# Fused transformer layer on one core: weight sums in place, side work spread over the attention stage, loads and stores begun a turn later

## The chip, the cores and the metric

The kernel is one launch on one core of a Trainium2 chip, written with a library that places tiles in pools, adds the semaphores and sets the order of instructions on each engine. Engines are named as in the profile: PE (matrix unit) and its weight loads (PEld), DVE (vector), ACT (scalar, activations), POOL (general purpose) and SP, whose queue issues nearly all DMAs. Each engine, and SP's queue, takes its instructions strictly in order: one that waits holds those behind it. The metric is the device time in microseconds (us), compared by the median of several runs.

## What is computed

One encoder layer over a sequence of 1024 positions of width 1024, in float32, with a conditioning vector c:

```python
mod = silu(c) @ w_ada + b_ada                    # six rows: sh1, sc1, g1, sh2, sc2, g2
h = layer_norm(x) * (1 + sc1) + sh1
q_a, k_a, v_a, f_a, q_c, k_c, v_c, gate_a, gate_c = split(h @ w_in)
o_a = forgetting_attention(q_a, k_a, v_a, f_a + b_f)      # 8 heads, causal
o_c = chunk_band_attention(q_c, k_c, v_c, rel_bias)       # 8 heads, a band of 9 chunks
mix = (sigmoid(gate_a) * (o_a @ w_br_fox) + sigmoid(gate_c) * (o_c @ w_br_chunk)) @ w_out
x = layer_norm(alpha * x + (1 + g1) * mix, ln1_g, ln1_b)
h = layer_norm(x) * (1 + sc2) + sh2
a, val = split(causal_depthwise_conv(h @ w_up, conv_w, conv_b))
x = layer_norm(alpha * x + (1 + g2) * ((silu(a) * val) @ w_down), ln2_g, ln2_b)
```

## The kernel before

Products in float32 are made of three matmuls: each operand is split into a rounded part and a remainder (`wh` and `wl` for weights; ACT makes `wh`, POOL makes `wl`, lines 103 and 104, from a loaded `ws`, line 96). The products with w_up and w_down are made with seven products of blocks instead of eight (Strassen's scheme), which needs sums and differences of weight blocks.

**The stage that the change touches** is attention, from about 114 us, when its first side loads are issued, to about 775 us. Eight pairs of heads are gone through in the order of a table `plan`: first the chunk branch (pairs 4 to 7), then the forgetting branch (2, 3, 0, 1). Per pair there are eight steps (two heads, four groups of queries): `scores` (PE `pss`, then DVE adds a bias and takes the minimum, line 477, then ACT's exponential, line 483), `probs` (PE transposes into `pst`, line 517; ACT and DVE split the result into two parts `pt`, lines 520 and 521), `weighted` (PE `pso`). `prep` readies the next head: it loads swapped key halves (`m2`, lines 420 and 421) and a bias tile. For the chunk branch this is `cb` (line 427), which DVE scales at once (line 428), and in which POOL then sets two corners; for the forgetting branch it is `fb` (line 424), from which POOL makes masked diagonal blocks `fm` (line 443).

Between these steps PE works on units of a `Stream`: projections of later heads (`psq`, `psv`) and the gates (`psg`, stored as `gd`). `step` advances the stream by about 2.6 us of PE work; one call is one turn.

Beside that run two generators, advanced a piece at a time:
- `beside`: the late modulation rows (`ada_late`, eight half rows). Each has eight pieces: load `wa` (256 KB, line 179), ACT multiplies by one value of the condition (183), POOL adds to `acc` (185), and at the end PE sums over partitions (`psada`).
- `aside`: `up_sums` for 8 pairs of blocks of w_up and `down_sums` for 11 pairs of rows of w_down, 19 units. Each loads two tiles `dr` of 512 KB (lines 567 and 550), POOL makes four sums or differences of 128x512 (573 and 555), and four stores of 256 KB go to scratch in HBM (`wd`, lines 576 to 578; `td`, lines 558 and 560). The later stages load them.

What sets the order: the library runs through the written order and places each instruction as early as its engine, its operands and its buffers let it by its own estimates, so that side work is often far ahead of where it is written. On the chip that order is fixed.

After the stage, `load_o` reads the attention outputs (`ost`), multiplies by inverted softmax sums (`ort`) and splits them (`oh`, ACT, line 758; `ol`, DVE, 759) for the merge with the gates (`psb`).

Of the kernel before, what the change touches and what calls it, by code (L numbers as in the profile page):

```python
# [42 lines left out]
def body(ctx, tc, a, out):  # L43
# [128 lines left out]
    def ada_late(v, half, pieces, accs, psum):  # L172

        acc = None
        ws = []
        for k in range(KD + 1):
            if k < KD:
                ws.append(pieces())
                sy.dma_start(out=ws[k], in_=ada_src(v, half * H, H)[:, k : k + 1, :])
            if k > 0:  # L180
                acc = acc or accs()
                w = ws[k - 1][:, 0, :]
                se.mul(out=acc if k == 1 else w, in_=w, mul=cond[:, k - 1 : k])
                if k > 1:
                    po.tensor_tensor(out=acc, in0=acc, in1=w, op=ALU.add)
            yield
        ps = psum()
        ada_sums(ps, acc, H)
        yield
        ada_bias(ps, v, half * H, H, v != 3)  # L190

# [57 lines left out]
    class Stream:  # L249
# [32 lines left out]
        def step(self):  # L282
            unit = self.units[self.cur]
            if self.gen is None:
                self.prime(self.cur)
                self.gen = unit.run(self.ready.pop(self.cur, []))
            cost = next(self.gen, None)
            if cost is None:
                self.live -= len(unit.parts)
                self.gen = None  # L290
                self.cur += 1
                cost = 0.0
            else:
                self.split()
            self.load()
            return cost
# [11 lines left out]
    qk = {}  # L308

# [85 lines left out]
    def unit_g():  # L395
        gi = next(gates)

        def run(ws):
            wh, wl = ws[0]
            for half in range(2):  # L400
# [8 lines left out]
                sy.dma_start(out=gd[half, gi], in_=sg)  # L409
# [128 lines left out]
    def mod(v, half):  # L538
        return ada_late(
            v, half, lambda: ap.tile([P, 1, H], F32, name=nm("wa"), tag="wa", bufs=2),  # L540
            lambda: ap.tile([P, H], F32, name=nm("acc"), tag="acc", bufs=1),
            lambda: pmm.tile([P, H], F32, name=nm("psada"), tag="mm"),
        )

    def down_sums():

        for i in range(NPAIR):
            rows = [ap.tile([P, D], F32, name=nm("dr"), tag=f"dr{r}", bufs=1) for r in range(2)]
            for r in range(2):
                sy.dma_start(out=rows[r], in_=a["w_down"][order[2 * i + r]])  # L550
            yield
            (b11, b12), (b21, b22) = [[w[:, halves(n)] for n in range(2)] for w in rows]
            t1, t3 = [ap.tile([P, H], F32, name=nm("dt"), tag=f"dt{r}", bufs=1) for r in range(2)]
            for j, (dst, x, y) in enumerate(((t1, b12, b11), (t3, b22, b12), (b22, b22, t1), (b21, b21, b22))):
                po.tensor_sub(out=dst, in0=x, in1=y)
                yield
                if j != 2:
                    sy.dma_start(out=td[i, (0, 2, 1, 3)[j]], in_=dst)
                    if j == 3:
                        sy.dma_start(out=td[i, 1], in_=b22)  # L560

    def up_sums():

        for c in range(HEAD):
            cols = [ap.tile([P, D], F32, name=nm("dr"), tag=f"dr{b}", bufs=1) for b in range(2)]
            for b in range(2):
                sy.dma_start(out=cols[b].rearrange("p (k n) -> p k n", k=KD), in_=a["w_up"][2 * c + b])
            yield
            (w11, w12), (w21, w22) = [[w[:, halves(n)] for n in range(2)] for w in cols]
            s1, s2 = [ap.tile([P, H], F32, name=nm("dt"), tag=f"dt{r}", bufs=1) for r in range(2)]  # L570
            for j, (dst, x, y, op) in enumerate(((s1, w21, w22, ALU.add), (s2, s1, w11, ALU.subtract),
                                                 (w11, w11, w21, ALU.subtract), (w12, w12, s2, ALU.subtract))):
                po.tensor_tensor(out=dst, in0=x, in1=y, op=op)
                yield
                if j in (0, 3):
                    sy.dma_start(out=wd[c, j], in_=dst)
            sy.dma_start(out=wd[c, 1], in_=s2)
            sy.dma_start(out=wd[c, 2], in_=w11)
# [111 lines left out]
    beside = chain(*(mod(v, half) for v in (2, 4, 3, 5) for half in range(2)))  # L690
    aside = chain(up_sums(), down_sums())
    ticks = 0
    for u, (ip, _) in enumerate(plan):
# [5 lines left out]
        for n in range(8 * u, 8 * u + 8):  # L699
# [3 lines left out]
            for qt in range(2):  # L703
# [17 lines left out]
            if i == 1 and g % 2 == 1:  # L721
                sy.dma_start(out=od[g // 2, ip], in_=o_now.pop((ip, g // 2)))
# [12 lines left out]
        if u % 2:  # L735
            inverted(ip - 1)
    for _ in chain(beside, aside):
        pass
# [7 lines left out]
    def load_o(half, pool, tag, bufs, rpool, rtag):  # L746
        os_ = {}
        for i in (4, 6, 2, 0):
# [13 lines left out]
        return os_  # L762

    o0 = load_o(0, ap0, "qs", 4, ap0, "m1")
    stream.finish(len(stream.units))
    es.close()
# [23 lines left out]
    def summed(c, j, pool, tag):  # L790
# [596 lines left out]
```

## Time and profile before

| | us |
|---|---|
| median of 3 runs | 1668.33 (1667.33 to 1672.18) |
| the profiled execution | 1665.98 |
| its span, first to last instruction | 1663.8 |
| PE busy | 1540.7 (93%) |
| DVE / ACT / POOL busy | 1041.0 / 790.8 / 593.4 |
| mean granted PE clock | 0.965 of full speed |
| DMA queue of SP | 264.42 MB, 47.3% of 16 engines' span |

Busy times of engines overlap, so they don't add up to the span. An engine's idle time counts only where the engine that sets the pace waits for it. In a row on a wait the engine named behind the arrow is the one whose event came last by the profile. The granted clock is what PE was given: at half clock a matmul takes almost twice as long. A DMA's time to landing runs from its issue to the arrival of all its data.

### The profile page before, as it was taken

The numbers are of one execution on the slowest core, as the hardware profiler recorded it, in microseconds if no ns is written. First come the engines' busy times: TensorE is split into PE (matmuls) and PEld (weight loads), VectorE is DVE, ScalarE is ACT, GpSimd is POOL, SyncE is SP. The second block draws the span as 40 slices with busy tenths as digits, with TensorE's granted clock in tenths as the row PEclk, the third lists the DMA queues.
The fourth block names the chain that finished last, engine by engine and source line by source line (L and its number), as shares of the span: only waits on it lengthen the run. The fifth ranks groups of instructions, "written<-read, shape, count | busy, mean of one in ns | idle before, by whom it ended". The sixth has DMA issues, their size and how long they took to land. (4 is left out here: it accounts for less than half of the span.)

```text
span 1663.8 us, 22257 instructions
## 1 busy us (share of the span) xinstructions
PE 1540.7 (93%) x7693; PEld 1290.5 (78%) x7693; DVE 1041.0 (63%) x2053; ACT 790.8 (48%) x1420; POOL 593.4 (36%) x455
## 2 busy tenths in 40 slices
PE   6899888887999999998889897899999999999996
PEld 3788777777988988887777675788888888888885
DVE  6746444434544545453758978577777877855688
ACT  3446544534555555553223535454544455456451
POOL 1126545645243242422204364545445445100000
PEclk9999989998999999999989898899999999999998
DMA  9037766676243244523763625443344232597552
GB/s 360 26 98 237 241 226 215 207 233 204 65 140 102 83 129 125 152 89 123 237 214 139 246 93 185 171 145 134 114 171 152 90 108 83 188 383 239 184 198 79
DMA packets 120449, 274.83 MB, mean 165 GB/s; under 512 B 12689, under 2 KB 21585, under 8 KB 120337
## 3 DMA queue, kind: packets, MB, share of 16 engines
q1 hardware_dynamic: 115056, 264.42, 47.3%
q10 hardware_dynamic: 4752, 7.17, 1.2%
q0 software_dynamic: 528, 1.84, 0.3%
q8 instruction: 60, 0.98, 0.2%
q14 instruction: 53, 0.43, 0.1%
HBM read 197.51 MB, written 67.47 MB: 159 GB/s over the span
## 5 line engine op out<-in xcount | busy, mean ns | idle before, releaser
L104 POOL TENSOR_TENSOR wl<-ws,wh 128x1024 fp32r<-128x1024 f32 x54 | 131.5, 2439 | 250.5 <-ACT wh L103 247.7
L816 PE MATMUL psu<-hc,wx 128*128 128x512 f32 x720 | 168.4, 389 | 0.0
L816 PEld LDWEIGHTS psu<-hc,wx 128*128 128x128 f32 x720 | 135.1, 188 | 28.1
L1052 DVE SCALAR_TENSOR_TENSOR pcv<-u,convp,pcv 128x1024 f32<-128x1024 f32 x88 | 113.2, 1286 | 45.4 <-ACT pcv L1050 44.4
L1193 DVE TENSOR_TENSOR op<-rw,op 128x512 fp32r<-128x512 f32 x146 | 93.5, 688 | 52.8 <-ACT op L1192 52.5
L1192 ACT CAST op<-rw 128x512 fp32r<-128x512 f32 x146 | 85.3, 622 | 83.1 <-PE psd L1205 39.5
L520 ACT CAST pt<-pst 128x512 fp32r<-128x512 f32 (+1 forms) x192 | 82.1, 451 | 74.1 <-PE pst L517 72.5
L521 DVE TENSOR_TENSOR pt<-pst,pt 128x512 fp32r<-128x512 f32 (+1 forms) x192 | 96.9, 520 | 30.0 <-ACT pt L520 28.4
L1204 PE MATMUL psd<-op,op 128*128 128x512 f32 x292 | 113.7, 389 | 0.9 <-DVE op L1193 0.9
L1203 PE MATMUL psd<-op,op 128*128 128x512 f32 x292 | 113.6, 389 | 0.0
L1205 PE MATMUL psd<-op,op 128*128 128x512 f32 x292 | 113.6, 389 | 0.0
L517 PE MATMUL pst<-ident,s 128*128 128x128 f32 x528 | 84.8, 280 | 28.5 <-DVE pt L521 28.5
L483 ACT ACTIVATE s<-s,mx 128x640 f32<-128x640 f32 (+7 forms) x128 | 94.4, 737 | 33.3 <-DVE mx L477 31.7
L228 PE MATMUL psq<-h1h,wl 128*128 128x512 f32 x256 | 103.9, 406 | 5.6 <-POOL wl L104 5.6
L226 PE MATMUL psq<-h1h,wh 128*128 128x512 f32 x256 | 107.6, 421 | 0.4 <-DVE h1h L222 0.4
L227 PE MATMUL psq<-h1l,wh 128*128 128x512 f32 x256 | 104.2, 407 | 1.8 <-DVE h1l L223 1.8
L226 PE MATMUL psg<-h1h,wh 128*128 128x512 f32 x256 | 105.3, 411 | 0.0
L228 PE MATMUL psg<-h1h,wl 128*128 128x512 f32 x256 | 101.0, 395 | 0.0
L227 PE MATMUL psg<-h1l,wh 128*128 128x512 f32 x256 | 100.9, 394 | 0.0
L531 PE MATMUL pso<-pt,vs 128*128 128x256 f32 x608 | 91.2, 288 | 4.2 <-DVE pt L521 3.1
L103 ACT CAST wh<-ws 128x1024 fp32r<-128x1024 f32 x54 | 56.3, 1046 | 76.7 <-PE psq L227 16.5
L517 PEld LDWEIGHTS pst<-ident,s 128*128 128x128 f32 x528 | 64.7, 144 | 35.3 <-DVE pt L521 28.5
(268 smaller groups left out, 4007.0 us busy)
## 6 DMA issues: line engine op xcount, KB each, us to landing
ws<-in_w_up SPq DMA_DIRECT2D x36, 512.0 KB, 3.7
wa<-in_w_ada SPq DMA_DIRECT2D x64, 256.0 KB, 3.3
dr<-in_w_down SPq DMA_DIRECT2D x22, 512.0 KB, 4.6
rw<-td SPq DMA_DIRECT2D x44, 256.0 KB, 4.6
yd<-y SPq DMA_DIRECT2D x20, 512.0 KB, 2.8
rw<-yd SPq DMA_DIRECT2D x40, 256.0 KB, 4.0
rw<-sd SPq DMA_DIRECT2D x33, 256.0 KB, 4.6
wa<-in_w_ada SPq DMA_DIRECT2D x8, 1024.0 KB, 10.8
```

Source lines behind the costliest of these rows:

```text
L104: po.tensor_sub(out=lo, in0=st, in1=hi)
L226: pe.matmul(ps, wh, xh, start=start, stop=False)
L227: pe.matmul(ps, wh, xl, start=False, stop=False)
L228: pe.matmul(ps, wl, xh, start=False, stop=stop)
L483: se.activation(out=st[:, 0:nk], in_=st[:, 0:nk], func=AF.Exp, scale=-1.0, bias=prev, accum_out=sums[:, col : col + 1])
L517: pe.transpose(ps[:, b * P : (b + 1) * P], st[:, c0 : c0 + P], ident)
L521: ve.tensor_sub(out=dl, in0=src, in1=dh)
L816: pe.matmul(ps, w[:, a_, k, :], h[k][b_], start=first, stop=k == 3 and a_ == 1, skip_group_check=on)
L1052: ve.scalar_tensor_tensor(out=ps, in0=u[b][:, 2 - d : S + 2 - d], scalar=cp[:, 2 - d : 3 - d], in1=ps, op0=ALU.mult, op1=ALU.add)
L1203: pe.matmul(ps[t], g[:, 0, ts], d[:, 0], start=start, stop=False, skip_group_check=on)
L1204: pe.matmul(ps[t], g[:, 0, ts], d[:, 1], start=False, stop=False, skip_group_check=on)
L1205: pe.matmul(ps[t], g[:, 1, ts], d[:, 0], start=False, stop=stop, skip_group_check=on)
```

## The change

- The sums of one unit are made in place in one tile `dr` of 128x4x512, by a common generator `four`; after the four sums one store of 1 MB takes all of it. The sums stand in another order in `wd` and `td`, and the readers' indices follow.
- `late_modulation` replaces `ada_late`: one generator over all 64 pieces, with loads issued two pieces ahead.
- Each turn advances both side generators (before, one of them), and both have turns in which nothing is issued, between a load and its first use and behind a store.
- Stores of gates (`gd`) and of attention outputs (`od`) are put on a list and issued at the next turn. In `step` the next weight's load comes ahead of the split of the one before, and both come a turn apart.
- Five mask buffers `fm` instead of three.
- `load_o` takes a list of pairs of heads; the last pair is read after the last gate unit.

```diff
             if cost is None:
...
                 cost = 0.0
+                self.load()
             else:
+                self.load()
                 self.split()
-            self.load()
             return cost
...
+    stores = []
+
+    def begun():
+        while stores:
+            stores.pop(0)()
...
-                sy.dma_start(out=gd[half, gi], in_=sg)
+                stores.append(partial(sy.dma_start, out=gd[half, gi], in_=sg))
...
-            fm = ap.tile([P, P], F32, name=nm("fm"), tag="fm", bufs=3)
+            fm = ap.tile([P, P], F32, name=nm("fm"), tag="fm", bufs=5)
...
+    def late_modulation():
+
+
+        pieces = [(v, half, k) for v in (2, 4, 3, 5) for half in range(2) for k in range(KD)]
+        ws = {}
+
+        def load(n):
+            if n < len(pieces):
+                v, half, k = pieces[n]
+                ws[n] = ap.tile([P, 1, H], F32, name=nm("wa"), tag="wa", bufs=2)
+                sy.dma_start(out=ws[n], in_=ada_src(v, half * H, H)[:, k : k + 1, :])
+
+        load(0)
+        yield
+        load(1)
+        yield
+        yield
+        for n, (v, half, k) in enumerate(pieces):
+            w = ws.pop(n)[:, 0, :]
+            if k == 0:
+                acc = ap.tile([P, H], F32, name=nm("acc"), tag="acc", bufs=1)
+                se.mul(out=acc, in_=w, mul=cond[:, 0:1])
+            else:
+                se.mul(out=w, in_=w, mul=cond[:, k : k + 1])
+                po.tensor_tensor(out=acc, in0=acc, in1=w, op=ALU.add)
+            yield
+            load(n + 2)
...
+            yield
+
+    def four(steps, srcs, dst):
+
+        x = ap.tile([P, 4, H], F32, name=nm("dr"), tag="dr", bufs=1)
+        for r in range(2):
+            sy.dma_start(out=x[:, 2 * r : 2 * r + 2, :], in_=srcs[r])
+        yield
+        yield
+        yield
+        for n, (o, p, q, op) in enumerate(steps):
+            po.tensor_tensor(out=x[:, o, :], in0=x[:, p, :], in1=x[:, q, :], op=op)
+            if n:
+                yield
+        sy.dma_start(out=dst.rearrange("j p n -> p j n"), in_=x)
+        yield
+        yield
...
-            t1, t3 = [ap.tile([P, H], F32, name=nm("dt"), tag=f"dt{r}", bufs=1) for r in range(2)]
-            for j, (dst, x, y) in enumerate(((t1, b12, b11), (t3, b22, b12), (b22, b22, t1), (b21, b21, b22))):
-                po.tensor_sub(out=dst, in0=x, in1=y)
-                yield
-                if j != 2:
-                    sy.dma_start(out=td[i, (0, 2, 1, 3)[j]], in_=dst)
-                    if j == 3:
-                        sy.dma_start(out=td[i, 1], in_=b22)
...
+            yield from four(((0, 1, 0, sub), (1, 3, 1, sub), (3, 3, 0, sub), (2, 2, 3, sub)), srcs, td[i])
...
                     spent += stream.step()
-                    ticks += 1
-                    if ticks % 2 or next(beside, aside) is aside:
-                        next(aside, None)
+                    begun()
+                    next(beside, None)
+                    next(aside, None)
...
-    o0 = load_o(0, ap0, "qs", 4, ap0, "m1")
+
+    o0, o1 = {}, {}
+    load_o(0, o0, (4, 6, 2), ap0, "qs", 4, ap0, "m1")
     stream.finish(len(stream.units))
+    begun()
+    load_o(0, o0, (0,), ap0, "qs", 4, ap0, "m1")
```

How the instructions stand on the engines at three places. First, SP around the load of the last chunk bias tile (`cb`), before and then after; a number at a name's end tells one buffer's use from another.

```order
L558 DMA td<-dr_6598 128x512
L550 DMA dr_6979<-in_w_down 128x1024
L722 DMA od<-o_521_2709 128x512
L550 DMA dr_6980<-in_w_down 128x1024
L558 DMA td<-dt_7020 128x512
L420 DMA m_709_3555<-qm_2891 64x1024
L409 DMA gd<-sg_3230 128x512
L96 DMA ws_3285<-in_w_v 128x1024
L421 DMA m_709_3555<-qm_2891 64x1024
L427 DMA cb_3558<-in_rel_t 128x640
L409 DMA gd<-sg_3302 128x512
L558 DMA td<-dt_7021 128x512
```

```order
L563 DMA dr_4862<-in_w_down 128x1024 x2
L295 DMA od<-o_514_2708 128x512
L571 DMA td<-dr_4862 128x4x512
L295 DMA gd<-sg_3225 128x512
L97 DMA ws_3298<-in_w_v 128x1024
L535 DMA wa_3390<-in_w_ada 128x512
L535 DMA wa_3505<-in_w_ada 128x512
L407 DMA m_699_3553<-qm_2886 64x1024
L295 DMA gd<-sg_3296 128x512
L408 DMA m_699_3553<-qm_2886 64x1024
L414 DMA cb_3556<-in_rel_t 128x640
L535 DMA wa_3603<-in_w_ada 128x512
```

Two modulation loads moved ahead of the bias load, and of the side work around it one store of 1 MB is left. On DVE the scaling of that tile stands here, before and after:

```order
L536 TENSOR_TENSOR o_573_2934<-pso_3309,ot_3322 64x256
L428 TENSOR_SCALAR cb_3558<-cb_3558 128x640
L521 TENSOR_TENSOR pt_3325<-pst_3335,pt_3325 128x4x128
L521 TENSOR_TENSOR pt_3326<-pst_3342,pt_3326 128x128
L477 ISA s_3361,mx_3365<-pss_3362,cb_3187 128x256
L477 ISA mx_3365 128x1
L521 TENSOR_TENSOR pt_3325<-pst_3369,pt_3325 128x3x128
```

```order
L523 TENSOR_TENSOR o_562_2928<-pso_3303,ot_3316 64x256
L508 TENSOR_TENSOR pt_3319<-pst_3329,pt_3319 128x4x128
L508 TENSOR_TENSOR pt_3320<-pst_3336,pt_3320 128x128
L464 ISA s_3356,mx_3360<-pss_3357,cb_3182 128x256
L464 ISA mx_3360 128x1
L508 TENSOR_TENSOR pt_3319<-pst_3364,pt_3319 128x3x128
L415 TENSOR_SCALAR cb_3556<-cb_3556 128x640
```

The scaling moved behind three evacuations of transposed scores (`pt`) and the score pass between them.

Second, SP at the last unit of the weight sums, before and after (`ws<-in_w_g` are gate weights, `fb<-fd` the bias tiles of the forgetting branch; the `fb` in the first piece is the second of eight, that in the second piece the third).

```order
L179 DMA wa_4683<-in_w_ada 128x512
L558 DMA td<-dr_7903 128x512
L560 DMA td<-dr_7903 128x512
L722 DMA od<-o_690_3463 128x512
L420 DMA m_893_4454<-qm_3642 64x1024
L421 DMA m_893_4454<-qm_3642 64x1024
L424 DMA fb_4457<-fd 128x1024
```

```order
L563 DMA dr_6788<-in_w_down 128x1024
L571 DMA td<-dr_6788 128x4x512
L563 DMA dr_7051<-in_w_down 128x1024 x2
L97 DMA ws_4566<-in_w_g 128x1024
L571 DMA td<-dr_7051 128x4x512
L411 DMA fb_4903<-fd 128x1024
L408 DMA m_980_4900<-qm_4503 64x1024
```

The last store of the sums moved from ahead of the second `fb` to ahead of the third, and the load of a unit's tile follows the store of the unit before.

Third, ACT at the end of the stage, before and after (`sg` the last two gates, `oh` the split of the last pair of attention outputs, `wh` weights of the merge).

```order
L408 ACTIVATE sg_7991<-psg_7966 128x512
L103 CAST wh_8104<-ws_8102 128x1024
L758 CAST oh_7962<-ost_7956 128x1024
L408 ACTIVATE sg_8019<-psg_7994 128x512
L103 CAST wh_8145<-ws_8143 128x1024
```

```order
L395 ACTIVATE sg_7867<-psg_7842 128x512
L104 CAST wh_7990<-ws_7988 128x1024
L395 ACTIVATE sg_7894<-psg_7869 128x512
L766 CAST oh_7904<-ost_7898 128x1024
L104 CAST wh_8031<-ws_8029 128x1024
```

The last gate moved ahead of the cast of the attention output.

More of the change, by code (lines that the diff above doesn't have):

```diff
@@ L1 @@
 import math
+from functools import partial
 from itertools import chain, count, cycle
@@ L536, in weighted @@
         ve.tensor_tensor(out=o32[own, g % 2 * 256 : (g % 2 + 1) * 256], in0=ps[own, 0:256], in1=tmp[own, :], op=ALU.add)
[L538 to L543, printed above, removed]
+    def late_modulation():
[21 more added lines that the diff above has]
+            load(n + 2)
+            if k == KD - 1:
+                ps = pmm.tile([P, H], F32, name=nm("psada"), tag="mm")
+                ada_sums(ps, acc, H)
+                yield
+                ada_bias(ps, v, half * H, H, v != 3)
+            yield
@@ L545, in down_sums @@
     def down_sums():
+        sub = ALU.subtract
         for i in range(NPAIR):
[L548 to L552, printed above, removed]
-            t1, t3 = [ap.tile([P, H], F32, name=nm("dt"), tag=f"dt{r}", bufs=1) for r in range(2)]
-            for j, (dst, x, y) in enumerate(((t1, b12, b11), (t3, b22, b12), (b22, b22, t1), (b21, b21, b22))):
-                po.tensor_sub(out=dst, in0=x, in1=y)
-                yield
-                if j != 2:
-                    sy.dma_start(out=td[i, (0, 2, 1, 3)[j]], in_=dst)
-                    if j == 3:
-                        sy.dma_start(out=td[i, 1], in_=b22)
+            srcs = [a["w_down"][order[2 * i + r]].rearrange("p (j n) -> p j n", j=2) for r in range(2)]
+            yield from four(((0, 1, 0, sub), (1, 3, 1, sub), (3, 3, 0, sub), (2, 2, 3, sub)), srcs, td[i])
@@ L562, in up_sums @@
     def up_sums():
+        sub = ALU.subtract
         for c in range(HEAD):
[L565 to L578, printed above, removed]
+            srcs = [a["w_up"][2 * c + b].rearrange("p (j k) n -> p j (k n)", j=2) for b in range(2)]
@@ L581, in body @@
+            yield from four(((3, 2, 3, ALU.add), (2, 0, 2, sub), (0, 3, 0, sub), (1, 1, 0, sub)), srcs, wd[c])
     plan = [
@@ L689, in body @@
     done = len(first_units)
-    beside = chain(*(mod(v, half) for v in (2, 4, 3, 5) for half in range(2)))
+    beside = late_modulation()
     aside = chain(up_sums(), down_sums())
-    ticks = 0
     for u, (ip, _) in enumerate(plan):
@@ L744, in body, with load_o @@
     o_cm, op_ = opened(name="o", bufs=1, side="right")
-    def load_o(half, pool, tag, bufs, rpool, rtag):
-        os_ = {}
-        for i in (4, 6, 2, 0):
+    def load_o(half, os_, pairs, pool, tag, bufs, rpool, rtag):
+        for i in pairs:
             st = pool.tile([P, 2, H], F32, name=nm("ost"), tag=tag, bufs=bufs)
@@ L788, in raw, with summed @@
         return raws[c, b]
-    def summed(c, j, pool, tag):
-        if (c, j) not in raws:
+    def summed(c, sl, pool, tag):
+        if (c, sl.start) not in raws:
             st = pool.tile([P, 2, H], F32, name=nm("ws"), tag=tag, bufs=2)
-            sy.dma_start(out=st, in_=wd[c, j : j + 2].rearrange("j p n -> p j n"))
-            raws[c, j] = [st[:, i, :].rearrange("p (k n) -> p k n", k=4) for i in range(2)]
-        return raws[c, j]
+            sy.dma_start(out=st, in_=wd[c, sl].rearrange("j p n -> p j n"))
+            raws[c, sl.start] = [st[:, i, :].rearrange("p (k n) -> p k n", k=4) for i in range(2)]
+        return raws[c, sl.start]
     def operand(slot, tmp, x, y=None, op=None, eng=ve, lo=po):
@@ L1013, in body @@
     turned_1(x1)
-    start = summed(order[0], 0, hbp, "fs"), raw(order[1], 1, hbp, "fs")
+    start = summed(order[0], slice(0, 4, 3), hbp, "fs"), raw(order[1], 1, hbp, "fs")
     g2row = g1p.tile([P, D], F32, name="g2row", tag="g1row")
```

30 lines of the change are left out of this document (7 added, 23 removed).

## Prediction

> **What bounds the kernel now.** I read the page first, then the busy time by stage, then PE's waits in the one stage where side work runs, then two of its stalls in order of time.
>
> ```profile
> span 1663.8 us, 22257 instructions
> PE 1540.7 (93%) x7693; PEld 1290.5 (78%) x7693; DVE 1041.0 (63%) x2053; ACT 790.8 (48%) x1420; POOL 593.4 (36%) x455
> PEclk9999989998999999999989898899999999999998
> ```
>
> PE is the bound, 1540.7 of 1663.8 us. What a rearrangement can win is PE's idle time, and the slow clock that shows up beside it. By stage (columns: length, then busy us of PE, PEld, DVE, ACT, POOL, then granted clock, DMA share, GB/s):
>
> ```profile
> 114.00:459.00 345.00, 304.31 (x1785) 268.90 (x1784) 164.82 (x488) 176.20 (x404) 179.76 (x148) 0.94 0.63 204
> 459.00:775.00 316.00, 310.56 (x1780) 270.09 (x1778) 151.95 (x456) 166.99 (x345) 103.93 (x101) 1.00 0.38 117
> 775.00:1050.00 275.00, 235.84 (x1002) 188.00 (x1003) 209.59 (x331) 107.10 (x147) 104.25 (x53) 0.91 0.52 178
> 1050.00:1664.00 614.00, 597.99 (x2636) 494.24 (x2634) 445.64 (x586) 294.50 (x449) 189.85 (x143) 0.99 0.47 165
> ```
>
> The attention stage is the first two rows. In its first 345 us PE idles 345.0 - 304.3 = 40.7 us, and a clock of 0.94 takes up to 0.06 x 345 = 20.7 us more; some of that falls on the idle time itself, so I count 14 (an estimate). So 55 us are to be had there. From 459 on PE is busy 310.6 of 316 us at full clock: nothing to win, and the side loads that still run there (DMA share 0.38) cost nothing. The 614 us after 1050 stay as they are. Who ends PE's idle time in the first 345 us (total us, times, longest):
>
> ```profile
> PE pst L517 <- DVE pt L521: 28.5, 7, 7.2
> PE psq L228 <- POOL wl L104: 5.6, 1, 5.6
> PE psv L323 <- POOL wl L104: 4.5, 2, 2.4
> ```
>
> DVE and POOL are only messengers. Two of the stalls, with SP's queue beside them (start, duration, in brackets the idle time before):
>
> ```profile
> 341.39 0.53 SPq L427 DMA_DIRECT2D cb<-in_rel_t  x1
> 345.24 5.69 SPq L550 DMA_DIRECT2D dr<-in_w_down  x2
> 348.00 0.49 DVE L428 TENSOR_SCALAR cb<-cb 128x640 f32<-128x640 f32 x1 [8.60 <-DMA cb<-in_rel_t]
> 349.27 1.33 PE L517 MATMUL pst<-ident,s 128*128 128x128 f32 x5 [7.23 <-DVE pt L521]
> 300.07 1.67 SPq L179 DMA_DIRECT2D wa<-in_w_ada  x2
> 302.84 0.72 ACT L183 ACTIVATE wa<-wa,cond 128x512 f32<-128x512 f32 x1 [6.26 <-DMA wa<-in_w_ada]
> 306.00 1.33 PE L517 MATMUL pst<-ident,s 128*128 128x128 f32 x5 [5.70 <-DVE pt L521]
> ```
>
> At 348 DVE stands at the scaling of a bias tile whose load has not landed, and the evacuation that PE needs is queued behind it. At 302.8 ACT stands in the same way at a modulation weight. Both loads are late on a queue that side work fills and blocks:
>
> ```profile
> SPq L558 <- POOL dt L555: 47.8, 19, 7.8
> SPq L550 <- DMA td<-dr: 14.6, 7, 4.7
> POOL dt L555 <- DMA dr<-in_w_down: 54.6, 14, 7.7
> ```
>
> SP waits 47.8 us to issue stores of sums that POOL has not made, 14.6 us until a store has landed and its buffer can be loaded again, and POOL waits 54.6 us for those loads, with the weight splits (wl) behind it. The side stream is too fast for what carries it, so it sets the pace.
>
> **The change, part by part. The weight sums.** Nineteen units (8 of w_up, 11 of w_down) stay, with the same bytes and the same four POOL sums; in place costs the same. The 76 stores become 19 of 1 MB; SP's DMAs fall from 731 to 674. What changes is the cycle of one unit:
>
> ```profile
> L567 SPq DMA_DIRECT2D dr<-in_w_up x16: 328/438/1182, 114.2 to 234.9; - x16
> L560 SPq DMA_DIRECT2D td<-dr x11: 319/423/477, 256.2 to 407.7; - x11
> L555 POOL TENSOR_TENSOR dr<-dr,dt x11: 1264/1292/1306, 253.0 to 399.4; 128x512 f32<-128x512 f32 x11
> dr<-in_w_down SPq DMA_DIRECT2D x22, 512.0 KB, 4.6
> sd<-sc SPq DMA_DIRECT2D x30, 256.0 KB, 2.3
> yd<-y SPq DMA_DIRECT2D x20, 512.0 KB, 2.8
> wa<-in_w_ada SPq DMA_DIRECT2D x8, 1024.0 KB, 10.8
> L104 POOL TENSOR_TENSOR wl<-ws,wh 128x1024 fp32r<-128x1024 f32 x17 | 40.5, 2388 | 24.6 <-ACT wh L103 24.6
> L185 POOL TENSOR_TENSOR acc<-acc,wa 128x512 f32<-128x512 f32 x29 | 37.2, 1284 | 26.4 <-ACT wa L183 22.9 <-ACT acc L183 1.6 <-issue 1.5
> ```
>
> Before: first load at 114.2, last store at 407.7, 293.5 us for 19 units, 15.4 each. Three of four stores left while later sums ran, and the first load of the next unit did not wait for them. After, nothing overlaps: one tile of one buffer is loaded, summed, stored, and loaded again when the store has landed. The unit's cycle c is then:
> - both loads: 4.6 to landing and 0.4 for the issue of the first, 5.0;
> - four sums of 1.29: 5.2;
> - POOL's other work between them: wl and acc are 77.7 us, at most 4.1 a unit and at least 0; POOL is idle half the time, so I take 2.0;
> - the store: 256 KB take 2.3 and 512 KB 2.8 us, so at least 2.8; the only 1 MB row is a crowded load at the start, 10.8, the upper end. Each 256 KB added costs 0.5 to 0.7 us there, and stores are nearer to stores: 4.0;
> - waits on SP ahead of that store and the next load: 0 to 3.3 (47.8 + 14.6 over 19); with 57 fewer entries, 1.0.
>
> That is 17.2 us, against 15.4.
>
> A page bears on the store alone: the Trainium skill, "DMA: Bandwidth & Descriptors", section on the anatomy of one DMA, fits 2.0 us plus bytes over 436 GB/s (to DMAs issued by the other path, GpSimd's). It gives 2.6 and 3.2 us where the rows show 2.3 and 2.8, and 4.4 for 1 MB; with 4.4 in place of 4.0 the sum below would win 22 us instead of 30.
>
> **Where this leaves PE.** In the new order of SP the last store stands between two loads which before issued at these times:
>
> ```profile
> 458.07 0.34 SPq L96 DMA_DIRECT2D ws<-in_w_g  x1
> 460.58 0.39 SPq L424 DMA_DIRECT2D fb<-fd  x1
> ```
>
> So the 19 units are laid beside 345 us of the old time line (114 to 459) instead of 293. Without stalls PE needs 345 - 55 = 290 us of it; the side stream needs 19 x 17.2 less the last landing, 327 - 4 = 323. The longer one decides, since SP is one queue and each load of the main work stands behind sums. At the end PE may run ahead, because there the main loads are early, while in the bias-tile part they are not:
>
> ```profile
> L427 SPq DMA_DIRECT2D cb<-in_rel_t x8: 422/537/730, 113.5 to 341.4; - x8
> L428 DVE TENSOR_SCALAR cb<-cb x8: 493/790/1571, 119.5 to 348.0; 128x640 f32<-128x640 f32 x8
> L424 SPq DMA_DIRECT2D fb<-fd x8: 383/506/616, 378.9 to 672.2; - x8
> L477 DVE CUSTOM_DVE_ANT_0 s<-pss,fb x56: 278/681/692, 432.3 to 744.3; 128x512 f32<-128x512 f32 x32, 128x128 f32<-128x128 f32 x8, 128x256 f32<-128x256 f32 x8, 128x384 f32<-128x384 f32 x8
> ```
>
> A bias tile of the chunk branch is wanted 6 us after its issue (119.5 - 113.5), the first one of the forgetting branch 53 us after (432.3 - 378.9). The lead lies between 0 and 48; the splits stand behind the sums on POOL with little lead, so I take 6. With the end of the stage (next part, 2 us), the saving is 345 + 4 - 19c + 6 + 2 = 357 - 19c, and at most 55 + 2. At c = 17.2 it is 30 us. On DVE the last bias scaling now stands behind three more evacuations, which agrees with a shorter stall there.
>
> **The output read in two parts.** In the new order ACT makes the last gate (sg) ahead of the last cast of the attention output (oh), after the weight cast that ended at 774.08:
>
> ```profile
> 773.04 1.04 ACT L103 CAST wh<-ws 128x1024 fp32r<-128x1024 f32 x1 [4.66 <-DMA ort<-rd]
> 777.67 1.04 ACT L758 CAST oh<-ost 128x1024 fp32r<-128x1024 f32 x1 [3.58 <-DVE ost L755]
> 778.62 0.59 ACT L408 ACTIVATE sg<-psg 128x512 f32<-128x512 f32 x1
> 779.27 0.79 PE L226 MATMUL psb<-oh,wh 128*128 128x512 f32 x1 [6.08 <-ACT sg L408]
> ```
>
> PE's wait of 6.08 us ends with sg, which could run 4.5 us earlier. But after twelve matmuls PE needs that oh, ready no earlier than now, and DVE and DMA waits follow to 1050. Between 0 and 4.5, I take 2.
>
> **At nothing.** Modulation weights: 64 loads, products and additions before and after, each load now issued two products ahead; bursts remain, and past 459 they lie under a PE that is 98% busy. Five mask buffers instead of three, stores of gates and outputs begun a turn later, weight loads ahead of splits: PE's waits name none of them, their cover is PE's own work, and the next to be late would be the split wl. The reordered rows of the stored sums: same bytes and same number of loads in the two later stages.
>
> **The sum.** The profiled execution took 1665.98 us (span 1663.8), 2.4 below the median of 1668.33. 30 us off it is 1636, off the median 1638: the forecast. It is c between 16.4 and 18.0, or 1623 to 1653.
>
> **Rivals.**
> 1. The side stream keeps up, c at or below 15.8 (store 3.3, other POOL work 1.3, SP waits 1.0 or less). For it: fewer DMAs compete for a share of 0.63. Against: the store's landing is new on the chain, and cannot be under 2.8. All 57 us: 1611. Chance 0.17.
> 2. The gain goes into the longer cycle, c from 18.5 to 19.05 (store 5.0, SP waits 1.5). For it: even SP's 5.69 us for two loads at 345 is a wait for stores of a quarter of the size. Within 5 us (0.3%, what a measurement here can tell from none): 1663 to 1673. Chance 0.10.
> 3. Slower: SP, standing at the next unit's load until the 1 MB store has landed, holds the bias loads behind it, and DVE stalls as at 348, once a unit. It decides from c = 19.05; with a store that lands in 6.0 us and SP waits of 1.4, c = 19.6 and 19 x 19.6 - 357 = 15 us are lost: 1683. Against: of the eight entries just ahead of the last bias load, the new order has three of side work (a store and two small loads), and no load that waits for a store. Chance 0.12. The same page of the Trainium skill, in the same section, says that a wait for a semaphore is held by the issuing sequencer ahead of dispatch, not by the DMA engines; by that rule this is where the loss would sit, and the 5.69 us row agrees.
> 4. The change does not spread anything: the new order still runs sums as early as buffers allow and modulation in bursts. That is so in both, and its effect is already in c; what is left of it (nothing gained, nothing lost) shares rival 2.
>
> **Chances.** The forecast (c from 15.8 to 18.5) 0.60, rival 1 0.17, rival 2 0.10, rival 3 0.12; 0.01 is left for another gain. Faster 0.78, same 0.10, slower 0.12. The range holds the forecast and rival 1: 1608 to 1668.
>
> **What would show it.** Right: in the stage's first part PE's idle time falls from 40.7 to some 20 us, waits of DVE for bias tiles and of ACT for wa shrink, the granted clock rises above 0.94; 19 stores land in about 4 us; the unit's cycle is near 17 us and the last store issues near 437; PE's first psb matmul waits under 3 us. Wrong: a store landing in 6 us or more, SP waiting for it longer than 2 us a unit, or PE waits that move past 459, where there were nearly none.

## The result and the profile after

| | before | changed |
|---|---|---|
| median, us | 1669.59 (1667.33 to 1672.18) | 1654.17 (1651.71 to 1658.46) |
| ratio of the runs, 95% interval | | 0.991 (0.9884 to 0.9936) |
| profiled execution, us (span) | 1665.98 (1663.8) | 1653.7 (1651.8) |

The change won 15 us by the medians and 12.3 us between the two profiled executions; 30 were forecast. The time lies in the range and on the side that was forecast, at half the size. The page of the changed kernel, its head and busy times:

```profile
span 1651.8 us, 22170 instructions
PE 1535.3 (93%) x7693; PEld 1286.5 (78%) x7693; DVE 1032.1 (62%) x2053; ACT 789.8 (48%) x1420; POOL 597.1 (36%) x455
```

The same stretches as before the change (length, busy us of PE, PEld, DVE, ACT, POOL, granted clock, DMA share, GB/s):

```profile
114.00:459.00 345.00, 308.21 (x1825) 272.30 (x1824) 165.73 (x501) 183.91 (x420) 189.98 (x157) 0.95 0.63 208
459.00:775.00 316.00, 309.86 (x1759) 269.22 (x1758) 152.10 (x447) 161.07 (x333) 98.84 (x93) 0.99 0.39 120
775.00:1050.00 275.00, 238.75 (x1032) 190.51 (x1031) 208.18 (x332) 111.25 (x157) 105.84 (x55) 0.94 0.54 185
```

In the first stretch PE still idles 345.0 - 308.2 = 36.8 us (40.7 before, some 20 forecast), at a clock of 0.95 (0.94). PE's waits there (us, times, longest) are the old ones, fewer and one of them longer:

```profile
PE pst L504 <- DVE pt L508: 20.4, 4, 10.2
PE pso L518 <- ACT pt L507: 7.0, 2, 4.4
PE psv L310 <- POOL wl L105: 3.6, 2, 2.8
```

Two of these stalls in the timeline (start, duration, in brackets the idle time before). First, DVE stands at the scaling of a bias tile, as before the change; then ACT stands at a modulation weight:

```profile
167.12 0.53 SPq L414 DMA_DIRECT2D cb<-in_rel_t  x1
172.89 0.49 DVE L415 TENSOR_SCALAR cb<-cb 128x640 f32<-128x640 f32 x1 [8.21 <-DMA cb<-in_rel_t]
174.16 1.33 PE L504 MATMUL pst<-ident,s 128*128 128x128 f32 x5 [6.83 <-DVE pt L508]
330.25 1.64 SPq L535 DMA_DIRECT2D wa<-in_w_ada  x2
336.21 0.72 ACT L548 ACTIVATE wa<-wa,cond 128x512 f32<-128x512 f32 x1 [11.03 <-DMA wa<-in_w_ada]
339.99 1.33 PE L504 MATMUL pst<-ident,s 128*128 128x128 f32 x5 [10.22 <-DVE pt L508]
```

The first of them can be followed back to POOL. Its sums wait 8.5 us for a load of `dr`, the split `wl` stands behind two of them, and SP can issue the next weight load (`ws`, at 166.18, 8.5 us late) and then the bias load only when that split is done:

```profile
161.12 2.66 POOL L568 TENSOR_TENSOR dr<-dr 128x512 f32<-128x512 f32 x2 [8.53 <-DMA dr<-in_w_up]
163.74 2.41 POOL L105 TENSOR_TENSOR wl<-ws,wh 128x1024 fp32r<-128x1024 f32 x1
166.18 0.33 SPq L97 DMA_DIRECT2D ws<-in_w_v  x1
```

The units and the forgetting branch, which serves as a mark of how far the main work is (min/median/max ns, first to last start in us):

```profile
L563 SPq DMA_DIRECT2D dr<-in_w_up x16: 328/426/1350, 114.3 to 250.3; - x16
L571 SPq DMA_DIRECT2D td<-dr x11: 377/377/427, 282.8 to 458.8; - x11
L464 DVE CUSTOM_DVE_ANT_0 s<-pss,fb x56: 278/676/692, 421.3 to 736.0; 128x512 f32<-128x512 f32 x32, 128x128 f32<-128x128 f32 x8, 128x256 f32<-128x256 f32 x8, 128x384 f32<-128x384 f32 x8
dr<-in_w_down SPq DMA_DIRECT2D x22, 512.0 KB, 4.5
td<-dr SPq DMA_DIRECT2D x11, 1024.0 KB, 4.5
```

The last store leaves at 458.8 (437 forecast). The branch begins 11.0 us earlier than before (421.3 against 432.3) and its scores end 8.3 earlier (736.0 against 744.3); the other 3.7 of the 12.0 us of span come later. What SP waits for in the first stretch:

```profile
SPq L571 <- POOL dr L568: 59.7, 15, 5.5
SPq L571 <- DMA dr<-in_w_down: 28.6, 7, 6.8
SPq L571 <- DMA dr<-in_w_up: 19.2, 4, 7.3
SPq L563 <- DMA td<-dr: 22.7, 7, 5.1
SPq L563 <- DMA wd<-dr: 17.5, 7, 5.6
```

Ahead of the store SP stands 107.5 us (59.7 for the sums, 28.6 and 19.2 for the loads ahead of them), and ahead of the next unit's load 40.2 us for the store to land (22.7 and 17.5), 2.1 a unit. Most of the queue's waiting is still for side work. The prediction left out the largest row of before, in which weight loads wait for the split `wl`. It stands here before and after:

```profile
SPq L96 <- POOL wl L104: 65.1, 16, 16.5
```

```profile
SPq L97 <- POOL wl L105: 35.2, 12, 8.5
```

Waits of ACT and of DVE for late loads in the same stretch:

```profile
ACT wa L548 <- DMA wa<-in_w_ada: 53.3, 20, 11.0
```

```profile
DVE cb L415 <- DMA cb<-in_rel_t: 17.8, 5, 8.2
```

Before, they were 38.7 and 18.3 us.

### The profile page after: what moved, and what is told of

Same layout as the page of the kernel before. It is cut to its first block, busy times and chain, and to the rows that moved or that the text cites. A ratio compares the mean times of both kernels' runs of the same rounds, so it can differ in the third digit from the quotient of the medians.

```text
span 1651.8 us, 22170 instructions
## 1 busy us (share of the span) xinstructions
PE 1535.3 (93%) x7693; PEld 1286.5 (78%) x7693; DVE 1032.1 (62%) x2053; ACT 789.8 (48%) x1420; POOL 597.1 (36%) x455
## 5 line engine op out<-in xcount | busy, mean ns | idle before, releaser
L568 POOL TENSOR_TENSOR dr<-dr 128x512 f32<-128x512 f32 x76 | 98.2, 1292 | 79.4 <-DMA dr<-in_w_down 48.1
L1213 PE MATMUL psd<-op,op 128*128 128x512 f32 x292 | 113.6, 389 | 0.0
L1215 PE MATMUL psd<-op,op 128*128 128x512 f32 x292 | 113.6, 389 | 0.0
L504 PE MATMUL pst<-ident,s 128*128 128x128 f32 x528 | 83.6, 278 | 20.5 <-DVE pt L508 20.4
L518 PEld LDWEIGHTS pso<-pt,vs 128*128 128x128 f32 x608 | 83.7, 194 | 19.4 <-ACT pt L507 11.2
```

Source lines behind the costliest of these rows:

```text
L518: pe.matmul(ps[:, 0:256], vs[:, h % 2, j0 + j, :], pt[j // 4][:, c, j % 4, :], start=j == 0 and c == 0, stop=j == nj - 1 and c == 1)
L568: po.tensor_tensor(out=x[:, o, :], in0=x[:, p, :], in1=x[:, q, :], op=op)
L1213: pe.matmul(ps[t], g[:, 0, ts], d[:, 0], start=start, stop=False, skip_group_check=on)
L1215: pe.matmul(ps[t], g[:, 1, ts], d[:, 0], start=False, stop=stop, skip_group_check=on)
```

## The experiments

Theory A is that of the prediction: the units' cycle on SP's queue sets the pace of the stage's first part. Each run has its own runs of before on the same chip, so versions are compared by their ratios to before. "Mark" is the shift of the forgetting branch's first and last score against 432.3 and 744.3, each in one profiled execution (that of before, 1665.98, was 3.6 below its median, so the marks show a few us too little).

| kernel | median, us | ratio to before (95%) | mark, us |
|---|---|---|---|
| changed | 1654.17 | 0.991 (0.9884 to 0.9936) | -11.0, -8.3 |
| e1: no sums | 1621.18 | 0.9686 (0.967 to 0.9702) | -48.0, -46.1 |
| e2: an eighth of the modulation | 1652.12 | 0.9875 (0.986 to 0.989) | -15.0, -11.3 |
| e3: dr loads held | 1638.22 | 0.9792 (0.9778 to 0.9807) | -42.0, -24.7 |
| e4: dr and wa loads held | 1638.42 | 0.9797 (0.9782 to 0.9811) | -38.5, -25.4 |
| e5: before, new sums alone | 1664.53 | 0.9945 (0.9929 to 0.996) | -13.4, -1.1 |
| e6: output read in one part | 1655.85 | 0.9894 (0.9877 to 0.9912) | -12.3, -7.5 |
| e7: before, dr loads held | 1659.17 | 0.9919 (0.9895 to 0.9942) | -23.9, -6.3 |
| e8: as e4, three wa buffers | 1638.48 | 0.9789 (0.9769 to 0.9809) | -38.6, -21.8 |
| e9: two more additions a unit | 1678.88 | 1.0061 (1.004 to 1.0082) | +6.1, +16.3 |
| e10: units in halves | 1649.31 | 0.9881 (0.9857 to 0.9904) | -15.5, -11.9 |
| e11: halves, loads held | 1623.16 | 0.9715 (0.9688 to 0.9743) | -47.7, -38.5 |
| e12: four stores | 1663.25 | 0.9949 (0.9931 to 0.9967) | -5.9, -1.1 |
| e13: before, new modulation alone | 1713.90 | 1.0243 (1.0215 to 1.0272) | -11.4, -10.1 |
| e14: one generator a turn | 1717.51 | 1.0267 (1.0244 to 1.029) | -8.2, -5.7 |

### e1 and e2: which side stream stalls PE

```diff
# e1
-            yield from four(..., srcs, td[i])     # and wd[c]
+            yield from ()
-            sy.dma_start(out=st, in_=wd[c, sl]...)
+            sy.dma_start(out=st, in_=a["w_up"][2 * c + sl.start]...)   # td: rows of w_down
# e2
-        pieces = [... for half in range(2) for k in range(KD)]
+        pieces = [... for half in range(2) for k in range(1)]
```

e1: 

> The changed kernel without the weight sums in the attention stage: no load of dr, no sums, no stores; the later stages read raw blocks of w_up and w_down of the same sizes in their place (so the output is another). The changed kernel took 1654; in the first part of the attention stage (114 to 459 us) its PE still idles 345.0 - 308.2 = 36.8 us, with further time at half clock. Theory A (the cycle of one unit, now 18.1 us, sets the pace of that part: what is left of the loss goes with it): the cap of my sum, 57 us below before in all, so 1611, and PE idles under 5 us there. Theory B (the remaining stalls come from loads of modulation weights and bias tiles that stand on SP behind splits and products, with the sums as a passenger): 1635 to 1654, with PE's stalls behind DVE pt and ACT pt still there.

e2: 

> The changed kernel with one piece of eight of each late half row of the modulation (8 loads of 256 KB, 8 products and no additions instead of 64, 64 and 56; the rows are so another value). Theory A: the weight-sum cycle loses only the additions of POOL between its sums (up to 37 us over the stage, some 1 us a unit) and a few waits of SP, c about 17, so 1654 - 19 = 1635 at best, 1640 likely. Theory B: the stalls behind ACT's products of wa go and the bias loads wait less: 1615 to 1630.

First stretch of e1, and PE's waits there in e2:

```profile
114.00:459.00 345.00, 334.19 (x2030) 296.07 (x2029) 183.88 (x556) 204.37 (x461) 111.38 (x98) 1.00 0.38 111
```

```profile
PE pst L504 <- DVE pt L508: 16.7, 3, 10.2
PE psq L209 <- POOL wl L105: 7.5, 2, 6.3
PE psv L310 <- POOL wl L105: 5.9, 2, 5.5
```

Each half row of e2 is padded with turns to the same 17 as before, so that the rest is spread over the same time. Without the sums PE idles 10.8 us there instead of 36.8, its clock stays at 1.00, and the time falls by 52 us against before (1 - 0.9686 of 1670). Theory A's cap of 57 us was 5 too high (1611 was written and 1621 measured, where before took 1672.7). Without seven eighths of the modulation the same kinds of stalls stay, and the interval overlaps that of the changed kernel. So the stream of sums stalls PE, and theory B falls.

But e2 was a miss for theory A too, which had written 1635 to 1640. The cycle did shorten, from 18.1 to (435.7 - 113.6) / 19 = 17.0 us (first load to last store), and the time fell by 2 us in the medians, 6 by the ratios. And e1 takes away the sums' traffic together with their place on SP's queue: a bias tile lands there in 3.7 us (median), in the changed kernel in 5.8. No run separates the two; in e3 it lands in 4.1 us and in e4 in 5.8, and both take the same time.

### e3, e4 and e8: the units held where they are written

The loads get an order edge behind the instruction that was written ahead of them on SP, so the library can't move them up.

```diff
# e3
-            sy.dma_start(out=x[:, 2 * r : 2 * r + 2, :], in_=srcs[r])
+            tc.keep_in_program_order(sy.dma_start(out=x[:, 2 * r : 2 * r + 2, :], in_=srcs[r]))
# e4: that, and
-                sy.dma_start(out=ws[n], in_=ada_src(...)...)
+                tc.keep_in_program_order(sy.dma_start(out=ws[n], in_=ada_src(...)...))
# e8: that, with three buffers of wa and
-            load(n + 2)
+            load(n + 3)
```

e3: 

> The changed kernel, all work kept, with the loads of dr held on SP behind everything written ahead of them, so that the units stand where they are written: the last store moves from beside 458 us of the time line of before to beside 693 us. Theory A: 19 units of 18 us are 344 us against some 580 us of main work, so the units no longer set anything: close to the case without sums, 1611 to 1620. Theory B: 42 of the 64 modulation loads still stand ahead of 459 us, and the stalls behind them stay: 1640 to 1654.

e4: 

> As the one with dr held, with the loads of the modulation weights wa held in their written places too (the last one beside 648 us instead of 608, and fewer bunches of six). Theory A: the same as with dr alone, within 5 us. Theory B: 10 us or more faster than with dr alone. A third way: loads that are held in written order stand on SP behind waits of the main work and reach ACT later, so that ACT's products stall PE more: slower than with dr alone by 5 us or more.

e8: 

> The changed kernel with dr and wa loads held in their written places, and three buffers of wa with loads three pieces ahead. With two buffers it took 1638, and one stall of 6.9 us at 625.7 stood behind ACT's product of a wa that landed 8.9 us after its issue, another of 5.7 at 210.7. If the lead of wa is what is short: both go, with their windows of half clock, 1625 to 1632. If not (DVE's bias tiles or the splits take their place): 1635 to 1640.

The same work, spread until 676.6 us instead of 458.8, takes 1638: the direction of theory A, but 18 us over e1 ((0.9792 - 0.9686) of 1670), where it said 1611 to 1620. The marks show where they are: the forgetting branch begins 6 us later than in e1 and then takes 329.3 us from the first to the last score (390.3 to 719.6), in e1 313.9 and before 312.0. The held units now stall PE there. Stretches of e3, to be compared with 310.6 us of PE at a clock of 1.00 before:

```profile
114.00:459.00 345.00, 329.52 (x1984) 291.15 (x1983) 182.88 (x545) 200.07 (x453) 162.85 (x137) 0.98 0.55 174
459.00:775.00 316.00, 299.82 (x1659) 259.25 (x1657) 148.65 (x416) 149.56 (x305) 134.57 (x115) 0.97 0.51 165
```

Holding wa as well changes nothing, and neither do three buffers for it. In e4 one of the stalls was this:

```profile
615.65 0.47 SPq L535 DMA_DIRECT2D wa<-in_w_ada  x1
624.63 0.72 ACT L548 ACTIVATE wa<-wa,cond 128x512 f32<-128x512 f32 x1 [8.19 <-DMA wa<-in_w_ada]
625.67 0.58 PE L518 MATMUL pso<-pt,vs 128*128 128x256 f32 x1 [6.92 <-ACT pt L507]
```

I took it for a short lead of wa. With three buffers a stall of 8.7 us stood at 637 in its place, behind DVE, which had stood 9.4 us for a load of `ort`. That reading failed.

### e5, e6, e12, e13, e14: the parts of the change

```diff
# e5: before, with four(), wd and td in the new order and their readers; mod() and turns as before
# e6: the changed kernel
-    load_o(0, o0, (4, 6, 2), ap0, "qs", 4, ap0, "m1")
+    load_o(0, o0, (4, 6, 2, 0), ap0, "qs", 4, ap0, "m1")
# e12: the changed kernel
-        sy.dma_start(out=dst.rearrange("j p n -> p j n"), in_=x)
+        for j in range(4):
+            sy.dma_start(out=dst[j], in_=x[:, j, :])
# e13: before, with late_modulation() in place of ada_late(); turns as before
# e14: the changed kernel
-                    next(beside, None)
-                    next(aside, None)
+                    ticks += 1
+                    if ticks % 2 or next(beside, aside) is aside:
+                        next(aside, None)
```

e5: 

> The kernel before with the weight sums alone changed (in place in one tile, one store of 1 MB, the readers' indices); modulation, turns, stores and the reading of the output as before. In its order the last store stands between 460.6 and 472 us of the time line of before, so the spreading comes from the single tile and its longer cycle, not from the turns. Theory A, with c = 18.1 as in the changed kernel: 7 to 12 us below before (1658 to 1663 against 1670). Theory B (what was won came from the modulation loads two ahead and the turns): within 3 us of before.

e6: 

> The changed kernel with all four pairs of heads of the output read in one go, ahead of the last gate unit, as before. I gave the split 2 us (0 to 4.5); the two time lines drew apart by 2.3 us between 765 and 790. Expected 1656 (1654 to 1659). Rival: PE finds the same wait behind another last cast or load, and it is worth nothing: 1654.

e12: 

> The changed kernel with four stores of 256 KB behind the fourth sum instead of one of 1 MB: 57 DMAs more. In its order the last store stands between 440 and 458 us. If the 1 MB store is what made the cycle longer than I worked out (4.9 us to landing, where 4.0 was taken): a landing in about 4 us, c 17.3, 10 us faster at the same place, or about the same with the earlier place: 1645 to 1655. If the number of DMAs counts (issue 0.4 each, and semaphores waited for): 1658 to 1668.

e13: 

> The kernel before with the late modulation alone changed (one generator, loads two pieces ahead; with the old turns its last load moves from beside 683 us to beside 769, and 26 of 64 loads stand ahead of 459 us where 36 did). I priced it at nothing: within 3 us of before. If it carries the 6 us that the sums alone don't explain: 4 to 8 us below before. If moving modulation out of the first part hurts the end of the stage: slower by 3 or more.

e14: 

> The changed kernel with one generator per turn, as before (the last store stands between 440.6 and 458 us, the last modulation load beside 769 us). If the turns carry the 6 us: 1660. If they carry nothing, since the library places both streams by buffers and not by turns: 1651 to 1657. If fewer modulation loads in the first part help there and cost nothing later: below 1650.

**e5**: 9 us of the 15 come with the sums alone, as theory A had it (its interval touches that of the changed kernel, 0.9929 against 0.9936, so that the other 6 are not certain). At the start of the forgetting branch the sums had won 13.4, at its end 1.1; one of the waits in between is that for a modulation weight on ACT:

```profile
475.38 0.72 ACT L183 ACTIVATE wa<-wa,cond 128x512 f32<-128x512 f32 x1 [3.54 <-DMA wa<-in_w_ada]
476.75 0.48 PE L517 MATMUL pst<-ident,s 128*128 128x128 f32 x1 [3.17 <-ACT s L483]
```

**e6**: reading the output in one part again costs nothing that can be measured. PE's wait at the last cast is not shorter with the split (first row, changed kernel) than without it (second row, e6, where a wait of 0.54 on `oh` comes first); before, it was 6.08:

```profile
771.21 0.80 PE L208 MATMUL psb<-ol,wh 128*128 128x512 f32 x1 [4.13 <-DVE ol L767]
```

```profile
770.31 0.77 PE L208 MATMUL psb<-ol,wh 128*128 128x512 f32 x1 [1.75 <-DVE ol L767]
```

**e12**: four stores a unit in place of one, 57 more DMAs, took 6.5 us more ((0.9949 - 0.991) of 1670), though each store landed in 2.1 us, SP stood 26.2 us for landings instead of 40.2, and the last store left 9 us earlier (450.0). So the store's landing alone was not what held the change back. The intervals just touch (0.9931 and 0.9936): that one store of 1 MB is better than four is likely, not certain. And the number of DMAs is not shown as the reason, since the new order also places the units up to 18 us earlier.

**e13 and e14**: the modulation alone makes the kernel before 41 us slower, and the changed kernel with the old turns takes 60 us more than with the new. Up to the end of the forgetting branch both had gained (-10.1 and -5.7); then PE waits for what is left of the modulation. The rows are the waits of e13 from 459 to 900 us and its stretches around the end of the stage:

```profile
PE psada L166 <- POOL acc L562: 55.8, 3, 19.9
```

```profile
700.00:775.00 75.00, 54.02 (x304) 46.96 (x303) 25.32 (x74) 30.12 (x60) 20.62 (x17) 0.86 0.34 109
775.00:850.00 75.00, 37.78 (x158) 31.34 (x159) 16.74 (x24) 23.29 (x30) 29.62 (x19) 0.71 0.42 124
```

`late_modulation` asks for two turns a piece, `ada_late` for one. With one generator a turn, in e14 as in e13, three half rows are still to be done when the attention is over, and each stands in PE's way for 18 to 20 us. The third outcome written for e13 had the place and not the size; none of those for e14 had it. One thing in e13 speaks against calling the modulation a mere passenger: with the old sums, and less of the modulation in the first part, the old units ended at 387.3 instead of 407.7 us, and the forgetting branch began 11.4 us earlier. That fits modulation work on SP and POOL that lengthens the units; it was not tried by itself.

### e7: the old units, held

```diff
-        sy.dma_start(out=st, in_=src)                  # load_w
+        mark[0] = sy.dma_start(out=st, in_=src).ins
...
+                with tc.issue_after(mark[0]):
                     sy.dma_start(out=rows[r], ...)     # and cols[b]
```

> The kernel before, all work and its 76 stores of 256 KB kept, with the loads of dr held on SP behind the newest load of a main weight: the units spread until the last store stands beside 745 us instead of 407. Theory A (the pace of the units is what stalled PE): as the changed kernel with its loads held, about 1640 (1632 to 1648). Rival C (fewer and larger stores are what helped, and the spread adds to it): 1650 to 1660. Rival D (units now run into the end of the stage, with late stores in the way of the output's loads): 1648 to 1665.

1659, a ratio of 0.9919: theory A's 1632 to 1648 was missed, and the time lies in the ranges of rivals C and D alike. The marks speak for D. At the start of the forgetting branch 23.9 us were won, at its end 6.3, as PE is stalled along the branch and not only at its end (7.6 of its 20.5 us of idle time after 459 lie before 560):

```profile
459.00:775.00 316.00, 295.52 (x1651) 255.58 (x1650) 141.16 (x428) 156.51 (x324) 146.40 (x133) 0.97 0.53 173
```

(Its profiled execution, 1665.91, was the slowest of four, the others 1657.6 to 1660.0; so the loss is seen a little too large.) The last store left at 755.9, and PE then waited 6.41 us for the last gate, as before. Holding the old units is worth 14 us (0.0081 of 1670), holding the new ones 19 against the changed kernel ((0.991 - 0.9797) of 1670, e4). The two edges are not alike, since the old units ran on until 755.9 us and the new ones until 675.8.

### e9, e10 and e11: the length of a unit

```diff
# e9, after the second and fourth sum
+                po.tensor_tensor(out=spare, in0=x[:, o, :], in1=x[:, o, :], op=ALU.add)
# e10
-        x = ap.tile([P, 4, H], F32, name=nm("dr"), tag="dr", bufs=1)
+        x = [ap.tile([P, 2, H], F32, name=nm("dr"), tag="dr", bufs=2) for _ in range(2)]
...
+            if n % 2:          # the half that is final leaves after the second sum
+                r = first if n == 1 else 1 - first
+                sy.dma_start(out=dst[2 * r : 2 * r + 2].rearrange("j p n -> p j n"), in_=x[r])
# e11: e10, with the loads of dr and wa held as in e4
```

e9: 

> The changed kernel with two more additions of 128x512 on POOL in each unit, into a tile that nobody reads, after its second and its fourth sum: c rises by 2 x 1.3 = 2.6 us, to 20.7; in its order the last store stands between 460.6 and 473.9 us of the time line of before, 3 to 14 later than in the changed kernel. Theory A in numbers (each microsecond of the cycle costs 19): 49 us more, less those 3 to 14, so 1689 to 1700, far slower than before. Rival E (the pace matters only where a main load stands behind a unit, and POOL's idle time takes the additions in): 1655 to 1670.

e10: 

> The changed kernel with the tile of a unit in two halves of 128x2x512, each with its own two buffers in turn; the half that is final after two sums is stored then (512 KB), the other after four, and each is loaded again when its own store has landed. Estimate of the cycle: 4.5 for the later half's load, 5.5 to the end of the sums, 0.4 + 3.5 for its store, 0.5 to the next load: 14.4, against 18.1. In its order the last store stands between 422 and 438 us, 20 to 36 earlier than in the changed kernel. Theory A in numbers: 19 x 3.7 = 70 us shorter, less 20 to 36, and at most to the cap: 1611 to 1625. Rival E (a faster unit is met by the same order of SP, and only splits and loads that stand behind it come earlier; the stalls of PE move): 1640 to 1655.

e11: 

> As the one in halves, with the loads of dr and wa held in their written places (last store beside 693 us). Held loads with one tile took 1638; without the sums 1621. If the unit's length still matters when it is spread (the part between load and last landing, about 17 us with one tile, some 13 here): 1625 to 1635. If what is left is only SP's queue and its order: 1636 to 1642.

Last stores of e9 and of e10 (the last start ends the units):

```profile
L574 SPq DMA_DIRECT2D td<-dr x11: 377/377/428, 294.8 to 490.1; - x11
```

```profile
L573 SPq DMA_DIRECT2D td<-dr x22: 370/378/1102, 252.4 to 415.0; - x22
```

In e9 the cycle rose to (490.1 - 114.9) / 19 = 19.7, by 1.6 and not by 2.6, and the kernel became 25 us slower than the changed one ((1.0061 - 0.991) of 1670): half of the 19 x 2.6 = 49, between the two theories. It is also slower than before, and its cycle lies past the limit of 19.05 in the prediction's third rival. In e10 the cycle fell to (415.0 - 114.0) / 19 = 15.8 (14.4 estimated), 44 us in all, and the time by 5, with intervals that overlap: rival E's number. The library places a shorter unit earlier, by 20 to 36 us here, which takes back most of what the cycle gives: 8 to 24 us should be left, and 5 were measured.

e11 fixes the place by hand and shortens the unit: 1623, ratio 0.9715, 48 us below before and 5 above e1, which does no sums at all. First stretch of e11, and DVE's waits for bias tiles there in e4 and in e11:

```profile
114.00:459.00 345.00, 337.94 (x2041) 298.72 (x2040) 185.34 (x557) 204.47 (x461) 167.38 (x143) 0.99 0.57 182
```

```profile
DVE cb L415 <- DMA cb<-in_rel_t: 14.0, 5, 5.9
```

```profile
DVE cb L415 <- DMA cb<-in_rel_t: 5.1, 5, 2.1
```

PE idles 7.1 us where it idled 36.8. Between e4 and e11 the bias tiles come sooner; that the 512 KB stores (2.8 us to landing against 4.4) are the reason was not tried by itself.

## Why the prediction was half right

**Direction and place: right.** The stream of sums set the pace of the first stretch (e1, e3), the stretch from 459 on was not disturbed (PE busy 309.9 of 316 us, 310.6 before), and the sums alone bring 9 of the 15 us (e5).

**The step that failed: the size of the cycle c.** By the prediction's own formula the time won is 357 - 19c. Measured, 19c = 458.8 - 114.3 = 344.5, c = 18.1, and the formula gives 12.5 us; the two profiled executions differ by 12.3. So c = 17.2 is where 18 us went. That the formula then comes within 0.2 us is in part luck: its lead of 6 us and the 2 us for the end of the stage were picked from wide bounds, and the marks show 11.0 us won at the start of the branch, 2.7 lost along it and 3.7 won behind it. The terms of c, as means over the units:
- both loads: 7.0 from the first issue to the second landing, where 5.0 stood. The second is issued 1.3 after the first, not 0.4 (in three units 2.6, 4.6 and 9.5 us after it, in the others 0.4 to 0.8), and each lands in 5.2, not 4.6: I had taken the median of one load for a pair.
- from there to the end of the sums: 5.5, where 5.2 + 2.0 stood. In most units of w_down the first sum begins before the second load has landed, and POOL's other work mostly fits between units.
- the store: 4.9 to landing, where 4.0 stood, and 0.4 + 0.6 of waits around it, as taken. (The means add up to 18.4; the last unit's store lies behind the end that c counts to.)

The page named in the prediction, the Trainium skill's "DMA: Bandwidth & Descriptors" (anatomy of one DMA), gives by its fit an estimate of 4.4 for 1 MB; the medians here are 4.5 and 4.7. By that price the prediction would have said 22 us, closer than 30.

**The step under it that failed: c as a price on its own.** Rival 1 said that c at or below 15.8 wins all 57 us. e10 has 15.8 and wins 20. A unit's length changes where the library puts the next one, and the formula held the last place fixed, at 459 us. With the measured cycle and the place that the last store has in each run's order, it gives these estimates, in us: e10, 19 to 35 (20 measured); e2, whose last store stands beside 441 to 458 us of the old time line, 17 to 34 (21 measured); e12, 2 to 20 (9 measured); e9, 3 to 17 lost (10 measured). The bounds are wide, and e5 falls outside: 17 to 28 without the 2 us for the output (9 measured; 13.4 were won at the start of the branch).

**Rival 3's mechanism was there.** SP stood 2.1 us a unit for the store's landing, just over the 2 that I had named as a sign against me. By the formula it did not make the kernel slower because c stayed below 19.05; e9, at 19.7, is slower than before. Rival 4 was half right too: the sums still run as early as the buffer allows, and that is what was left to win (e3, e11). But the prediction also said that side loads past 459 us cost nothing. That held for what ran there in the changed kernel, not for held units, which stall the branch (e3, e7).

**Signs that failed.** PE's idle time in the first stretch is 36.8 us, not some 20, and the last store leaves at 458.8, not 437. DVE's waits for bias tiles did not shrink (18.3 to 17.8 us), ACT's for wa grew (38.7 to 53.3). PE's first psb wait is 4.1, not under 3; the 2 us for the split output are not shown (e6).

**"At nothing".** The modulation's DMAs and products are indeed worth little (e2: 2 to 6 us, with intervals that overlap). But its cover was not PE's work alone: it was the turn of its own that the change gives it. Taken away, it costs 41 to 60 us (e13, e14), and I had not named it.

Still open: the 6 us that the sums alone don't explain, and whether the sums hurt more by their place on SP and POOL or by their traffic. Modulation and turns can't be had singly, and the loads and stores begun a turn later were not tried alone.

## What to carry to other kernels

- Side work that is written beside the main work need not run there: read from the trace where it stands on its queue. If it is bunched at the front, hold it by an order edge. Against the changed kernel that brought 20 us with one line (e3), and 33 together with units in halves (e11). What is held stalls the later part a little: look there as well (e3, e7).
- A longer or shorter unit is not a price by itself when a scheduler places the next one by it. Take its length and its new place from the new order together.
- An edit priced at nothing has a cover; ask which other line of the same change provides it, and what happens without (e13, e14).

## What the runs showed of the hardware

Stores from one tile land in 2.1 us for 256 KB, 2.8 for 512 KB and 4.5 for 1 MB, medians to landing (e12, e11, and the changed kernel above):

```profile
td<-dr SPq DMA_DIRECT2D x44, 256.0 KB, 2.1
```

```profile
td<-dr SPq DMA_DIRECT2D x22, 512.0 KB, 2.8
```

Fourfold size, about twice the time. The kernel with four stores of 256 KB a unit took 6.5 us more than that with one of 1 MB, with intervals that just touch (e12).
